# A one-core decoder block on Trainium2: spilled data returned on GpSimd's queue, arithmetic taken off GpSimd, one FFN granule split earlier

## The chip, the cores and the metric

The kernel runs on one core of a Trainium2 chip. The metric is device time in microseconds (us) from the start of the program to its end. Engines are named as in the profile: PE is TensorE (matrix products), PEld its weight loads, DVE is VectorE, ACT is ScalarE, POOL is GpSimd, SP is SyncE, which here only issues transfers. SP, ACT and POOL each have a queue of their own for transfers.

## The reference, cut to what matters

One decoder block in float32 for 512 tokens of width 2048, batch 1: native sparse attention (16 heads of 128, four key/value groups, a compressed, a selected and a sliding-window branch, gated), then a SwiGLU feed-forward net (FFN) of inner width 5632, each behind an RMSNorm, with residual adds and a final RMSNorm.

```python
for i in range(DEPTH):                       # DEPTH = 1
    hn = rmsnorm(h, mix_norm_g[i])
    h = h + nsa_mixer(hn, ...)               # proj = hn @ w_in; ...; o @ w_out
    h = h + swiglu(rmsnorm(h, ffn_norm_g[i]), ffn_w_in[i], ffn_w_out[i])
return rmsnorm(h, final_norm_g)

def swiglu(h, w_in, w_out):
    z = h @ w_in
    a, b = z[..., :D_FF], z[..., D_FF:]
    return (jax.nn.silu(a) * b) @ w_out
```

## The kernel before, in words

**A product.** Every float32 operand is split in two halves: `hi`, its rounded float32r copy, and `lo`, the rest. `three` (L285 to L287) makes one product of three matmuls, hi·hi (L285), one lo with hi (L286), one hi with lo (L287). In a profile row such as `proj<-whi,hn_l` the operands stand behind the arrow.

**Weights** come in granules of 512 KB (128 partitions x 1024 numbers). The class `Weights` keeps three steps apart. `load` (L79) issues the transfer into one of three buffers `raw`, on the queue that `W.queue` names: SP, but POOL while the attention heads run. `split` writes `whi` on ACT (L95) and `wlo`, by a subtraction, on DVE (L99), or on GpSimd when the granule's number is in `on_pool`. The halves go to one of four conversion buffers or, for granules in `W.place`, to a slot of `wr_h`/`wr_l`, which hold them for good. `ahead(n)` splits until n granules stand ready beyond those that PE has taken, and loads up to three more; `take` hands the next one to the matmuls. A raw buffer is filled again only when both parts of its split are done.

**Order.** The order on every engine is the order in which the program calls the instructions; nothing is moved later. Each engine runs its own list in order, and an instruction that waits holds what is behind it on that engine. A transfer's issue counts as such an instruction on the engine whose queue it uses.

**Stages.** (1) First norm and the first projections. (2) The attention heads: `steps(h)` is a list of a head's steps with their places, run between pieces of a second stream, `dense()`, which makes the projections of the coming heads (`qpair`, `kpair`, `vpair`) and then, `N_SPILL` = 6 times, `partial(cb)`: a block of 256 columns of the output projection over heads 0 to 11, added to the input x and stored to DRAM (`d_h`, L722, on POOL). In a head, `turn` transposes the probabilities (L772) into a buffer `turned` and stores it as `d_p` (L773; for the last token tile also `d_pc`, L775); `fetch` reads it back rearranged as `pt` (L779); `part_hi` and `part_lo` split it (L798, `ptl` L808); `values` multiplies it with the value vectors (`o<-ptl,v1h`). The outputs of heads 0 to 10 are stored in DRAM (`d_o`); `reload_o(i)` (L701) brings back four heads (three for i = 2) into `hn_h` and `hn_l`, once the last `qpair`, that of heads 14 and 15, is through with granule i and the place is free.

(3) When the heads are done, `acc`, the residual of 4 token tiles x 2048 columns, is filled: the last 512 columns from x (L890), the first 1536 from `d_h` (L891, 3 MB). `gb2`, the second norm's weights on all partitions (1 MB), is loaded on ACT's queue (L912). The last 512 columns of the output projection over heads 0 to 11 are then made in one block, with `w_out` granules of 2 heads x 512 columns. (4) Token tiles t = 0 to 3: heads 12 to 15 for the four column blocks `cb`, with eight granules split once at t = 0 and held (`w8`; the first six in `wr_h`/`wr_l`). Each block is added to `acc` on DVE (`add`, L895), which frees PE's bank; ACT squares it (L942) into a throw-away bank of PSUM; `rstd` (L230 to L241) makes the norm's factor from the sums; `scaled` multiplies `acc` by factor and `gb2`, three blocks of 512 columns on DVE (L252), the fourth on ACT (L254) and GpSimd (L255). `turned` transposes the tile before this one on PE (L263) and splits the result (`hn_h` on ACT L269, `hn_l` on DVE L274). At a tile's end `W.ahead(min(t, 2))` splits coming granules.

(5) The FFN: three column blocks of 256 plainly (`pp` banks; granules of its first block are numbers #8 to #11 counted from the first held one), during which sums for the rest are prepared; the others as seven products on half-sized blocks (`products`, banks `f0` to `f3`, L1083 on); and the FFN's output projection (L1372 on).

## Time and profile before

| | us |
|---|---|
| median of 3 runs | 2139.99 (2139.48 to 2142.34) |
| the profiled execution | 2138.04 |
| its span, first to last instruction | 2136.2 |
| PE busy in it | 2103.8 (98 %) |
| DVE busy | 1578.0 (74 %) |
| ACT busy | 1001.6 (47 %) |
| POOL busy | 159.8 (7 %) |
| mean granted PE clock | 0.995 |

How to read the views: the page gives busy time per engine over the whole span. A row of the waits is "engine, line, tile <- releaser: us in total, times, longest". A row of the timeline is "start, duration, engine, line, operation, out<-in, shape", and in brackets the engine's idle time before it and what ended that. A row of the chain of waits is "start, duration, what". Matmul rows overlap, since they are pipelined; the spacing of their starts is what one costs. A row such as `raw<-in_nsa_w_out SPq` is a transfer on SP's queue; its last number is the time from issue to landing.

### The profile page before, as it was taken

To read this page: it belongs to the slowest core of one execution; us is meant where nothing else is said; L and a number is where in the kernel's file an instruction comes from. 1 tells how busy PE (TensorE), PEld (TensorE's weight loads), DVE (VectorE), ACT (ScalarE), POOL (GpSimd) and SP (SyncE) were. 2 spreads that over 40 slices of the span, in tenths; PEclk is the share of its full clock that TensorE was granted. 3 is DMA by queue.
4 is the path that set the end of the run, shared out by engine and by line. 5 is a ranking of instruction groups with operands and counts; after the bars stand their busy time and mean duration, and the time that the engine had idled before them with its cause. 6 is when DMAs were issued, how large, how long until landed. Compare 5 with 4: busy or idle time off the path is not lost.

```text
span 2136.2 us, 37530 instructions
## 1 busy us (share of the span) xinstructions
PE 2103.8 (98%) x14821; PEld 1955.8 (92%) x14821; DVE 1578.0 (74%) x2560; ACT 1001.6 (47%) x1629; POOL 159.8 (7%) x233
## 2 busy tenths in 40 slices
PE   8999999999999999999999999999999999999997
PEld 6888898888989978899999999999999888999996
DVE  5565667666656356898888888888888787877776
ACT  5344666666746244444344343443434444444344
POOL 1000111111111121000000000000000000000000
PEclk9999999999999999999999999999999999999999
DMA  6555577766886742343343343443433876878784
GB/s 209 177 159 164 157 201 195 200 187 183 244 259 191 244 161 105 122 139 122 126 130 127 121 126 122 129 129 119 127 121 119 282 277 220 310 262 315 288 312 149
DMA packets 258732, 391.38 MB, mean 183 GB/s; under 512 B 27467, under 2 KB 183163, under 8 KB 257916
## 3 DMA queue, kind: packets, MB, share of 16 engines
q1 hardware_dynamic: 230912, 272.55, 40.6%
q0 software_dynamic: 25648, 112.01, 15.6%
q10 hardware_dynamic: 1996, 4.42, 0.6%
q8 instruction: 116, 1.90, 0.4%
q14 instruction: 60, 0.49, 0.1%
HBM read 323.28 MB, written 70.88 MB: 185 GB/s over the span
## 4 chain that ended last, share of the span: by engine, by line
PE 92%; DVE 3%; DMA 2%; ACT 1%; issue 1%; POOL 0%; ACTq 0%; DVEq 0%; SPq 0%; POOLq 0%
PE f L287 19%; PE f L286 19%; PE f L285 19%; PE proj L285 9%; PE proj L286 8%; PE proj L287 8%; PE o L286 1%; PE o L287 1%; PE s L285 1%; PE o L285 1%; PE s L287 1%; PE s L286 1%; DVE wlo L99 1%; DMA raw<-in_nsa_w_out 1%; DMA d_pc<-turned 1%
## 5 line engine op out<-in xcount | busy, mean ns | idle before, releaser
L99 DVE TENSOR_TENSOR wlo<-raw,whi 128x1024 fp32r<-128x1024 f32 (+1 forms) x223 | 270.3, 1215 | 83.9 <-ACT whi L95 83.8
L95 ACT ACTIVATE whi<-raw 128x1024 fp32r<-128x1024 f32 (+1 forms) x226 | 233.9, 1039 | 200.9 <-DVE raw L968 124.2
L968 DVE TENSOR_TENSOR tlo<-tt,thi 128x1536 fp32r<-128x1536 f32 (+2 forms) x134 | 195.9, 1462 | 110.8 <-ACT thi L1070 88.7
L285 PE MATMUL f<-hn_h,whi 128*128 128x256 f32 x984 | 271.7, 276 | 0.8 <-ACT E L1028 0.8
L287 PE MATMUL f<-hn_h,wlo 128*128 128x256 f32 x984 | 271.6, 276 | 0.0
L286 PE MATMUL f<-hn_l,whi 128*128 128x256 f32 x984 | 271.6, 276 | 0.0
L1065 ACT ACTIVATE whi<-raw 128x1024 fp32r<-128x1024 f32 x123 | 126.1, 1057 | 292.3 <-DVE raw L968 282.1
L285 PE MATMUL proj<-hn_h,whi 128*128 128x512 f32 x512 | 202.8, 396 | 0.3 <-ACT hn_h L419 0.3
L286 PE MATMUL proj<-hn_l,whi 128*128 128x512 f32 x512 | 199.9, 390 | 0.3 <-DVE hn_l L420 0.3
L287 PE MATMUL proj<-hn_h,wlo 128*128 128x512 f32 x512 | 199.9, 390 | 0.0
L285 PEld LDWEIGHTS f<-hn_h,whi 128*128 128x128 f32 x984 | 184.7, 188 | 1.3 <-ACT E L1028 1.3
L287 PEld LDWEIGHTS f<-hn_h,wlo 128*128 128x128 f32 x984 | 184.7, 188 | 0.0
L286 PEld LDWEIGHTS f<-hn_l,whi 128*128 128x128 f32 x984 | 184.7, 188 | 0.0
L285 PE MATMUL proj<-whi,hn_h 128*128 128x256 f32 (+2 forms) x568 | 163.5, 288 | 0.0
L287 PE MATMUL proj<-whi,hn_l 128*128 128x256 f32 (+2 forms) x568 | 162.9, 287 | 0.0
L286 PE MATMUL proj<-wlo,hn_h 128*128 128x256 f32 (+2 forms) x568 | 162.8, 287 | 0.0
L1070 ACT ACTIVATE thi<-tt 128x1536 fp32r<-128x1536 f32 x82 | 121.9, 1487 | 84.0 <-PE f L286 84.0
L968 DVE TENSOR_TENSOR wlo<-raw,whi 128x1024 fp32r<-128x1024 f32 x123 | 147.0, 1223 | 0.0
L287 PE MATMUL f<-whi,tlo 128*128 128x512 f32 x320 | 124.9, 390 | 0.6 <-DVE tlo L968 0.6
L286 PE MATMUL f<-wlo,thi 128*128 128x512 f32 x320 | 125.0, 391 | 0.0
L285 PE MATMUL f<-whi,thi 128*128 128x512 f32 x320 | 124.7, 390 | 0.0
L287 PEld LDWEIGHTS proj<-hn_h,wlo 128*128 128x128 f32 x512 | 96.1, 188 | 21.4 <-DVE wlo L99 0.2
(323 smaller groups left out, 6157.6 us busy)
## 6 DMA issues: line engine op xcount, KB each, us to landing
raw<-in_ffn_w_in SPq DMA_DIRECT2D x135, 512.0 KB, 3.6
raw<-in_ffn_w_out SPq DMA_DIRECT2D x88, 512.0 KB, 5.6
rawx<-in_ffn_w_in SPq DMA_DIRECT2D x41, 512.0 KB, 4.9
rawx<-d_a SPq DMA_DIRECT2D x34, 512.0 KB, 4.9
ah<-d_s POOLq DMA_DIRECT2D x16, 896.0 KB, 7.0
al<-d_s POOLq DMA_DIRECT2D x16, 896.0 KB, 9.1
raw<-in_nsa_w_in SPq DMA_DIRECT2D x24, 512.0 KB, 4.4
raw<-in_nsa_w_in POOLq DMA_DIRECT2D x24, 512.0 KB, 6.1
```

The source lines that it names most:

```text
L95: self.nc.scalar.activation(hi[:, :n], src, AF.Copy)
L99: eng.tensor_tensor(lo[:, :n], src, hi[:, :n].bitcast(F32), op=OP.subtract)
L285: mm(o, ah, bh, start=start, stop=False, skip_group_check=True)
L286: mm(o, ah, bl, start=False, stop=False, skip_group_check=True)
L287: mm(o, al, bh, start=False, stop=stop, skip_group_check=True)
L968: dve.tensor_tensor(o, a, b, op=OP.subtract)
L1065: act(h, r, AF.Copy)
L1070: act(h, ttf, AF.Copy)
```

## The change

1. `reload_o` issues its six transfers on POOL's queue, not SP's, and each pair is called inside the next granule of the last `qpair`, behind its second step.
2. `acc<-d_h` (3 MB) and `gb2` (1 MB) are loaded on POOL's queue, behind the last store of `d_h`; before, on SP's and ACT's.
3. GpSimd does no arithmetic: `on_pool` is gone (all low halves are made on DVE), and `scaled` does all four blocks on DVE.
4. `wr_h`/`wr_l` have seven slots, so that one granule fewer takes a conversion buffer. `W.ahead` at the end of tile t gets (0, 1, 3, 3)[t] instead of (0, 1, 2, 2)[t]: the third FFN granule (#10) is split after t = 2.
5. PSUM: the pool `psx` stays to the end; products and output projection take their first bank from it and f1 to f3 from `pf` (`ffn_banks`).

PE's instructions are the same in number and order; only names of banks and buffers differ. The lines of the changed file are up to 8 lower.

SP's transfers at the end of the last `qpair` before. `d_p_93<-turned_1828` is the store of transposed probabilities of one token tile, `pt` the read back:

```order
L701 DMA hn_h<-d_o 128x4x512
L701 DMA hn_l<-d_o 128x4x512
L773 DMA d_p_93<-turned_1828 128x512
L779 DMA pt_1833<-d_p_94 32x4x64 x4
L773 DMA d_p_92<-turned_1827 128x768
L779 DMA pt_1832<-d_p_93 32x4x128 x4
L701 DMA hn_h<-d_o 128x3x512
L701 DMA hn_l<-d_o 128x3x512
L773 DMA d_p_91<-turned_1826 128x1024
```

and POOL's queue there now (`stage` and `tb` are loads for the first spilled block and for a head's bias):

```order
L694 DMA hn_h<-d_o 128x4x512
L694 DMA hn_l<-d_o 128x4x512
L79 DMA raw<-in_nsa_w_out 128x4x256
L694 DMA hn_h<-d_o 128x4x512
L694 DMA hn_l<-d_o 128x4x512
L79 DMA raw<-in_nsa_w_out 128x4x256
L694 DMA hn_h<-d_o 128x3x512
L694 DMA hn_l<-d_o 128x3x512
L79 DMA raw<-in_nsa_w_out 128x4x256
L700 DMA stage<-in_x 128x4x256
L636 DMA tb<-d_u 128x512
```

The third pair stood on SP directly ahead of a tile's `d_p` (and `d_pc` behind it); now each pair stands on POOL between two raw loads.

DVE from the last spilled block to the first two adds of tile t = 0, before:

```order
L720 TENSOR_TENSOR stage<-stage,proj 128x512
L99 TENSOR_TENSOR wlo<-raw,whi 128x1024 x4
L99 TENSOR_TENSOR wr_l<-raw,wr_h 128x1024 x3
L895 TENSOR_TENSOR acc<-acc,proj 128x512 x2
L895 TENSOR_TENSOR acc<-acc,po 128x512 x2
L99 TENSOR_TENSOR wlo<-raw,whi 128x1024
L895 TENSOR_TENSOR acc<-acc,proj 128x512 x2
```

and now:

```order
L713 TENSOR_TENSOR stage<-stage,proj 128x512
L98 TENSOR_TENSOR wlo<-raw,whi 128x1024 x4
L98 TENSOR_TENSOR wr_l<-raw,wr_h 128x1024 x6
L888 TENSOR_TENSOR acc<-acc,proj 128x512 x2
L888 TENSOR_TENSOR acc<-acc,po 128x512 x2
L98 TENSOR_TENSOR wr_l<-raw,wr_h 128x1024
L98 TENSOR_TENSOR wlo<-raw,whi 128x1024
L888 TENSOR_TENSOR acc<-acc,proj 128x512 x2
```

Six splits of held granules stand ahead of the adds of the column block, where three stood; the other three were on POOL.

DVE from the multiplies of tile t = 2 into t = 3, before:

```order
L252 SCALAR_TENSOR_TENSOR xn<-acc,rs,gb_7617 128x512 x3
L895 TENSOR_TENSOR acc<-acc,proj 128x512 x2
L274 TENSOR_TENSOR hn_l<-pp,hn_h 128x4x128 x2
L895 TENSOR_TENSOR acc<-acc,po 128x512
L274 TENSOR_TENSOR hn_l<-pp,hn_h 128x4x128 x2
```

and now:

```order
L247 SCALAR_TENSOR_TENSOR xn<-acc,rs,gb_7617 128x512 x4
L98 TENSOR_TENSOR wlo<-raw,whi 128x1024 x2
L888 TENSOR_TENSOR acc<-acc,proj 128x512 x2
L266 TENSOR_TENSOR hn_l<-pp,hn_h 128x4x128 x2
L888 TENSOR_TENSOR acc<-acc,po 128x512
```

A fourth multiply and two splits (granules #9 and #10) now stand ahead of the adds of tile t = 3.

The diff:

```diff
--- before.py
+++ after.py
@@ -65,7 +65,7 @@
     def __init__(self, nc, raw, conv, specs):
         self.nc, self.raw, self.conv, self.specs = nc, raw, conv, specs
         self.nd = self.ncv = self.nt = 0
-        self.r, self.c, self.place, self.on_pool, self.sums = {}, {}, {}, set(), {}
+        self.r, self.c, self.place, self.sums = {}, {}, {}, {}
         self.at, self.off = 0, {}
         self.queue, self.late = nc.sync, None
 
@@ -93,10 +93,9 @@
         src = self.r.pop(i).rearrange("p k c -> p (k c)")
         rest = self.sums[i](src) if i in self.sums else None
         self.nc.scalar.activation(hi[:, :n], src, AF.Copy)
-        eng = self.nc.gpsimd if i in self.on_pool else self.nc.vector
 
         def low():
-            eng.tensor_tensor(lo[:, :n], src, hi[:, :n].bitcast(F32), op=OP.subtract)
+            self.nc.vector.tensor_tensor(lo[:, :n], src, hi[:, :n].bitcast(F32), op=OP.subtract)
 
         if self.late is None:
             low()
@@ -193,13 +192,10 @@
     dram = ctx.enter_context(tc.tile_pool(name="dram", bufs=1, space=DRAM))
     front, early = ctx.enter_context(ExitStack()), ctx.enter_context(ExitStack())
     hnp = front.enter_context(tc.tile_pool(name="hnp", bufs=1))
-    psx = early.enter_context(tc.tile_pool(name="psx", bufs=2, space=PSUM))
+    psx = ctx.enter_context(tc.tile_pool(name="psx", bufs=2, space=PSUM))
     specs, specs2, marks, off = granules(w_in, w1k, w1v, w_out, f_in, f_out)
     W = Weights(nc, rawp, convp, specs)
     W.at, W.off = 48, off
-    for m in marks:
-        W.on_pool.update((m + 1, m + 3, m + 5, m + 7))
-    W.on_pool.update((marks[0] + 9, marks[0] + 11))
 
     ident = const.tile([128, 128], F32, name="ident")
     make_identity(nc, ident)
@@ -245,14 +241,10 @@
         run(rstd_steps(ss, y))
         return y
 
-    def scaled(src, y, gb, dst, n_pool):
+    def scaled(src, y, gb, dst):
         for j in range(4):
             c = slice(512 * j, 512 * (j + 1))
-            if j < 4 - n_pool:
-                dve.scalar_tensor_tensor(dst[:, c], src[:, c], y, gb[:, c], op0=OP.mult, op1=OP.mult)
-            else:
-                act(dst[:, c], src[:, c], AF.Copy, scale=y)
-                pool.tensor_tensor(dst[:, c], dst[:, c], gb[:, c], op=OP.mult)
+            dve.scalar_tensor_tensor(dst[:, c], src[:, c], y, gb[:, c], op0=OP.mult, op1=OP.mult)
 
     def transposed(xn, js, tiles):
         ps = []
@@ -664,9 +656,10 @@
             ps = proj2()
             end = q_out(ps, h0)
             for i in range(4):
-                yield from ws(ps, i, W.take(), end=end)
-                if h0 == H - 2 and i < 3:
-                    reload_o(i)
+                for k, _ in enumerate(ws(ps, i, W.take(), end=end)):
+                    if h0 == H - 2 and i and k == 1:
+                        reload_o(i - 1)
+                    yield
 
         def kpair(g):
             ps = proj2()
@@ -698,8 +691,8 @@
         def reload_o(i):
             n = min(4, N_BACK - 4 * i)
             for part, t in enumerate((hn_h, hn_l)):
-                nc.sync.dma_start(t[:, 4 * i:4 * i + n].bitcast(F32),
-                                  d_o[4 * i:4 * i + n, part].rearrange("h p s -> p h s"))
+                pool.dma_start(t[:, 4 * i:4 * i + n].bitcast(F32),
+                               d_o[4 * i:4 * i + n, part].rearrange("h p s -> p h s"))
 
         def partial(cb):
             st = ap_.tile([128, 1024], F32, name="stage").rearrange("p (t c) -> p t c", t=NT)
@@ -888,7 +881,7 @@
     acc = accp.tile([128, NT, D], F32, name="acc")
     spill = 256 * N_SPILL
     nc.sync.dma_start(acc[:, :, spill:], x[:, spill:].rearrange("(t p) c -> p t c", p=128))
-    nc.sync.dma_start(acc[:, :, :spill], d_h.rearrange("(t p) c -> p t c", p=128))
+    pool.dma_start(acc[:, :, :spill], d_h.rearrange("(t p) c -> p t c", p=128))
 
     def add(t, cb, p):
         a = acc[:, t, 512 * cb:512 * (cb + 1)]
@@ -909,11 +902,11 @@
     with tc.tile_pool(name="n2", bufs=1) as n2:
         act(warm, epsc, AF.Sqrt)
         gb2 = n2.tile([128, D], F32, name="gb2")
-        nc.scalar.dma_start(gb2, ffn_g[0:1, :].to_broadcast([128, D]))
+        pool.dma_start(gb2, ffn_g[0:1, :].to_broadcast([128, D]))
         xn = n2.tile([128, D + 64], F32, name="xn")
-        wr_h = n2.tile([128, 6, 1024], F32R, name="wr_h")
-        wr_l = n2.tile([128, 6, 1024], F32R, name="wr_l")
-        for i in range(6):
+        wr_h = n2.tile([128, 7, 1024], F32R, name="wr_h")
+        wr_l = n2.tile([128, 7, 1024], F32R, name="wr_l")
+        for i in range(7):
             W.place[marks[0] + i] = wr_h[:, i], wr_l[:, i]
         for cb in range(N_SPILL // 2, 4):
             po = out_tiles()
@@ -940,8 +933,8 @@
                     turned(xn, (2 * cb - 2, 2 * cb - 1), t - 1)
                 junk = ps3.tile([128, 512], F32, name="pp")
                 act(junk, acc[:, t, 512 * cb:512 * (cb + 1)], AF.Square, accum_out=ss[:, cb:cb + 1])
-            scaled(acc[:, t], rstd(ss), gb2, xn, 1)
-            W.ahead(min(t, 2))
+            scaled(acc[:, t], rstd(ss), gb2, xn)
+            W.ahead((0, 1, 3, 3)[t])
         pa = [ps3.tile([128, 512], F32, name="pp") for _ in range(2)]
         gs = []
         for i in range(4):
@@ -1083,8 +1076,7 @@
     def products(q):
         p, u = q // 2, q % 2
         if not u:
-            banks[p] = [pf.tile([128, 512], F32, name=f"f{i}").rearrange("p (a c) -> p a c", a=2)
-                        for i in range(4)]
+            banks[p] = [x.rearrange("p (a c) -> p a c", a=2) for x in ffn_banks()]
         order = ("p1", "p5", "p2", "p3", "p7", "p6", "p4") if p else ("p1", "p5", "p2", "p7", "p6", "p4", "p3")
         for n in order:
             bh, bl = prod[q][n]
@@ -1157,6 +1149,10 @@
             sub(hn_l[:, k, T2], S4[u], f32(hn_h[:, k, T2]))
     early.close()
     pf = ctx.enter_context(tc.tile_pool(name="pf", bufs=2, space=PSUM))
+
+    def ffn_banks():
+        return [psx.tile([128, 512], F32, name="proj")] + [pf.tile([128, 512], F32, name=f"f{i}")
+                                                           for i in range(1, 4)]
 
     W2 = Weights(nc, rawp, convp, specs2)
     pool.memset(tp.tile([128, TP_GAP], F32, name="gap", bufs=1), 0.0)
@@ -1372,8 +1368,8 @@
     n, na, pending = 0, 1, None
     for b in range(4):
         units = ORDER[b][:-N_TAIL] if b == 3 else ORDER[b]
-        po = [pf.tile([128, 512], F32, name=f"f{i}") for i in range(4)]
-        qs = {x: pf.tile([128, 512], F32, name=f"f{i}") for i, x in enumerate(("p1", "p5", "p6", "p7"))}
+        po = ffn_banks()
+        qs = dict(zip(("p1", "p5", "p6", "p7"), ffn_banks()))
         first7 = next(j for j in units if j in SEVEN[b])
         last7 = [j for j in units if j in SEVEN[b]][-1]
         started = False
```

## The prediction

> **What bounds the kernel now.** First the page's busy shares, then TensorE's list of waits: if TensorE (PE) is nearly full, only its waits can be won.
>
> ```profile
> PE 2103.8 (98%) x14821; PEld 1955.8 (92%) x14821; DVE 1578.0 (74%) x2560; ACT 1001.6 (47%) x1629; POOL 159.8 (7%) x233
> ```
> ```profile
> PE o L286 <- DVE ptl L808: 4.8, 1, 4.8
> PE proj L285 <- issue: 3.2, 1, 3.2
> ...
> PE pp L287 <- DVE wlo L99: 2.7, 1, 2.7
> PE f L285 <- ACT E L1028: 0.8, 1, 0.8
> ...
> PE pp L263 <- DVE hn_l L274: 0.4, 1, 0.4
> ```
> PE is 98 % busy and the change removes no matmul. Four single waits, here called A (4.8), B (3.2), C (2.7) and D (0.8), stand where the diff works. A wait costs more than its idle time: in the windows view (us, then busy time of PE, PEld, DVE, ACT, POOL, then PE's granted clock) the next stretch runs at half clock after A, B and C:
>
> ```profile
> 605.60:609.06 3.46, 1.21 (x11) 1.00 (x9) 0.00 (x0) 0.00 (x0) 0.00 (x0) 1.00 1.03 337
> 609.06:615.88 6.82, 4.32 (x20) 4.32 (x21) 3.58 (x13) 3.38 (x8) 0.76 (x1) 0.50 0.64 171
> 762.66:766.07 3.41, 3.41 (x9) 2.65 (x9) 1.69 (x4) 1.20 (x2) 2.41 (x1) 0.50 0.62 202
> 820.68:824.10 3.42, 0.84 (x7) 0.85 (x8) 3.42 (x3) 0.36 (x1) 1.44 (x1) 1.00 0.00 0
> 824.10:827.51 3.41, 3.41 (x19) 3.41 (x18) 0.30 (x1) 0.00 (x0) 0.00 (x0) 0.50 0.92 303
> ```
> PE's timeline around A, and the chain of waits in the half-clock stretch, give the spacing of like matmuls:
>
> ```profile
> 605.73 0.28 PE L287 MATMUL proj<-whi,hn_l 128*128 128x256 f32 x1
> ...
> 606.53 0.28 PE L285 MATMUL o<-pth,v1h 128*128 128x256 f32 x1
> 611.56 0.58 PE L286 MATMUL o<-ptl,v1h 128*128 128x256 f32 x1 [4.75 <-DVE ptl L808]
> ```
> ```profile
> 615.21 0.21 PE proj L286
> 615.42 0.21 PE proj L287
> ```
> Full clock: seven steps in 0.80, 0.114 each. Half clock: 0.21, so 1−0.114/0.21 = 46 % of busy half-clock time is lost. A: 611.56−606.53−0.114 = 4.92 late, which is 0.17 over its idle time; I add 0.17 to the other waits too. Half clock after A: 4.32×0.46 = 1.99; after B and C 3.41×0.46 = 1.57 each. So **A = 6.91, B = 3.37+1.57 = 4.94, C = 2.87+1.57 = 4.44, D = 0.97**, together 17.26.
>
> **Part by part.** *Reload of hn (A).* SP's timeline, the chain, the DMA table (last column: median us to landing) and DVE's timeline:
>
> ```profile
> 596.03 0.38 SPq L701 DMA_DIRECT2D hn_h<-d_o  x1
> ```
> ```profile
> 597.52 13.11 DMA d_pc<-turned
> ```
> ```profile
> d_pc<-turned SPq DMA_DIRECT2D x16, 64.0 KB, 2.8
> ```
> ```profile
> 610.72 0.48 DVE L772 STREAM_TRANSPOSE turned<-p 128x288 f32<-128x288 f32 x1 [7.05 <-DMA d_pc<-turned]
> ```
> The third reload pair (3 heads, 1.5 MB) goes out directly ahead of the 512 KB d_p and the 64 KB d_pc on SP. d_pc lands after 13.11 instead of 2.8; the transpose that reuses its buffer waits, then ptl, then PE. The transpose sat idle 7.05 and PE lost 4.92, so A is gone if d_pc lands 4.92 earlier, by 605.7, in 8.2. On POOL the pair follows this raw load:
>
> ```profile
> 593.01 0.75 POOL L79 DMA_DIRECT2D raw<-in_nsa_w_out  x1 [9.04 <-DVE turned L772]
> ```
> so it goes out at about 593.8, three us before d_p. From 593 POOL's queue then has two raw blocks (1 MB), the pair (1.5), a stage (0.5) and a tb (0.25): 3.25 MB. At the 337 GB/s of the first window that ends at 602.7; if all of it went ahead of SP, d_p and d_pc (0.58 MB, 1.7 us) would land at 604.4 (6.9 us); if SP gets half, at 601 (3.4). Both are under 8.2. I take A as gone. The three pairs are six more issues on POOL, of 0.75 or less by the row above, on a queue that sat idle 9 us there. Each pair waits until PE has finished a granule of qpair, and stands behind a raw load that comes after that, so it holds nothing up: the raw loads queued behind it are for granules well ahead of PE. The first partial block needs the third pair's heads only in its last granule, some 12 us after 593.8. If this cover fails, PE waits for the pair itself, at most as long as for d_pc now.
>
> The Trainium skill speaks against this edit: DMA: Bandwidth & Descriptors ("Issuing engines are not separate DMA queues") says that DMAs started from any engine share the same 16 engines, so that another issuer saves only issue time. By it the bytes still collide and A stays (a rival below); the trace's stall, though, is order within one queue, which the move does change.
>
> *acc<-d_h and gb2 (B).* From the chain of waits and DVE's timeline:
>
> ```profile
> 736.47 0.35 ACTq L912
> ...
> 740.41 11.64 DMA raw<-in_nsa_w_out
> ```
> ```profile
> 760.37 1.23 DVE L99 TENSOR_TENSOR wr_l<-raw,wr_h 128x1024 fp32r<-128x1024 f32 x1 [3.60 <-ACT wr_h L95]
> 761.52 1.28 DVE L895 TENSOR_TENSOR acc<-acc,proj 128x512 f32<-128x512 f32 x2
> ```
> ACT stands on gb2's issue and SP on acc<-d_h's until the last spilled block has landed at 736.4; then 4 MB run ahead of the raw loads. The sixth place granule (raw #5) ends at 761.6, and the adds that free PE's banks stand behind its split.
>
> With both loads on POOL, nothing on ACT or SP waits for d_h. The splits then go as PE frees conversion buffers, one granule (48 matmuls×0.114 = 5.5 us) after the other: I place them at 727, 732 and 737.5, and the raw loads #0 to #4 that take the emptied raw buffers between 730 and 742. What is new is that these share the engines with POOL's 4.2 MB (3 MB of acc, 1 MB of gb2) from 737:
>
> ```profile
> DMA packets 421, 2.53 MB, mean 422 GB/s; under 512 B 9, under 2 KB 9, under 8 KB 420
> ```
> ```profile
> q0 software_dynamic: 291, 1.19, 97.5%
> q1 hardware_dynamic: 17, 0.03, 3.0%
> ```
> ```profile
> q0 software_dynamic: 134, 0.55, 67.6%
> q1 hardware_dynamic: 133, 0.27, 35.0%
> ```
> The first is 741.5 to 747.5, the others 1678 to 1681 and 1681 to 1683, where POOL (q0) loads beside SP (q1). If the queues alternate packets as in the last pair, SP has 0.27 MB in 2 us, 135 GB/s: raws #2 to #4, from 740, take 3.9 us each until 751.5, and #5, with the engines to itself from 752.3 (POOL's 4.2 MB at 275), lands at about 753.5. If POOL's bytes all go first (737 to 747 at 422), four raws of 0.52 MB follow in 5.0, with about 2 us to landing: 754. My estimate is between. It must land by 755.9: ACT 1.06, DVE 1.23 and an add of 0.68 later (1.28 for two) is 758.9, when PE wants the bank. B is gone at both ends, with about 2 us to spare; against it, six splits now precede the adds on DVE, three before, and a wait there holds every later split, add and multiply.
>
> *No arithmetic on GpSimd, third granule early (C, t=2).*
>
> ```profile
> 819.83 3.38 DVE L99 TENSOR_TENSOR wlo<-raw,whi 128x1024 fp32r<-128x1024 f32 x1
> ```
> ```profile
> 819.60 2.52 POOL L99 TENSOR_TENSOR wlo<-raw,whi 128x1024 fp32r<-128x1024 f32 x1 [0.24 <-POOL xn L255]
> ```
> C is the third granule's split on DVE, which took 3.38 instead of the 1.23 of the row at 760.37, while GpSimd split another granule. The third granule is now split a tile earlier, and the fourth, behind t=3's multiplies, finds GpSimd idle and ends on DVE 2.1 earlier than 823.2, ahead of PE: C is gone. The moved multiply is free for the same reason:
>
> ```profile
> L252 DVE SCALAR_TENSOR_TENSOR xn<-acc,rs,gb x12: 744/750/1784, 778.1 to 818.1; 128x512 f32<-128x512 f32 x12
> ```
> ```profile
> 804.12 3.11 DVE L252 SCALAR_TENSOR_TENSOR xn<-acc,rs,gb 128x512 f32<-128x512 f32 x3
> ```
> The third multiply takes 1.78 beside GpSimd's; the two before take 3.11−1.78 = 1.33, 0.67 each, so four alone take 2.75 with the pipeline's end, less than 3.11. The 0.4 wait at t=2 should shrink by 0.3.
>
> *What it adds: t=3.* Two splits (1.1 to 1.2 each) now stand on DVE between t=2's multiplies and the adds: xn ends at 806.9, the splits at 809.1, two adds at 810.4, and by my estimate the Square at 810.6 and hn_l's first half at 811.9. PE wants these banks for its second transposes:
>
> ```profile
> 810.05 1.03 PE L263 MATMUL pp<-ident,xn 128*128 128x128 f32 x8
> ```
> The first four need a bank free at 810.6, the next one at 812 against 810.5. Below nothing it cannot go (no wait stands there now); above, 3 us if the delay of the splits (2.4) and of the banks add. I take 1.5, between, since the matmuls behind can start when one bank is free. Half clock would add 1.57: A, B and C had under 1.3 us of work in 3.41, and a 1.5 us wait leaves 1.9; the 0.8 of D was followed by none.
>
> The Trainium skill, TensorE: Matmul & The Clock Gate ("Why this matters for your kernels"), puts the drop at gaps over about 3 us; C's 2.7 tripped it, so the rule is too loose here, and the row decides. By the rule t=3 would stay at 1.5 even at the upper bound.
>
> *PSUM (D).* The first product's bank was the one that ACT's E had still to empty; now it is one free since the token tiles. The third product, 1.4 later, needs ACT's at about the time it is ready: D is gone, between 0 and 0.97; I take 0.97.
>
> **Sum.** −17.26−0.3+1.5 = **−16.1**. Against the profiled execution's own 2138.04 (span 2136.2, 1.84 around it) that is 2121.9; the runs' median, 2139.99, is 1.95 above it, which gives **2124**. Later, PE stays the bound and splits run 1 to 3 us ahead of it, so the gain reaches the end. All small bounds together (t=3 from 0 to 4.6, D from 0.97 to 0): 2122 to 2128, the forecast's own range.
>
> **The rivals.**
> R1, B stays: six splits or POOL's 4 MB make raw #5 late by the spare 2 plus 3.4. For: the 97.5 % row. Against: ACT starts 10 us earlier. 2124+4.9 = 2129.
> R2, A stays: POOL's packets hold d_p and d_pc beyond 8.2. For: 6.9 at the one end leaves 1.3. Against: 3.4 at the other. 2124+6.9 = 2131.
> R3, the waits only move (the change doesn't do what it says): A and B stay and t=3 costs 3: 2124+6.9+4.9+1.5+1.57 = 2139.
> R4, slower: POOL's loads go ahead of SP's and are slow themselves, as
>
> ```profile
> acc<-d_r POOLq DMA_DIRECT2D x1, 2048.0 KB, 13.0
> ```
> has 157 GB/s. Then 4.2 MB end at 763.7, raw #2 lands at 765, is split by 767.3, and raw #5 (0.52 MB, 3.3 us at that rate) takes its buffer and lands at 770.6: 14.7 late, and 1.6 of half clock. At A, 3.25 MB end at 613.7: 8+2. Time 2124+16.3+10 = 2150. With raw #5 after 770.3 the change is, at B alone, no longer faster. Against it: in the 97.5 % row POOL moved 1.19 MB in 3 us, 397 GB/s.
>
> **How the numbers follow.** Forecast 0.60 (2124), R1 0.15 (2129), R2 0.12 (2131), R3 0.08 (2139), R4 0.05 (2150). A measurement tells some 0.2 % (4.3 us) from no change: the first three are faster, 0.87; R3 the same, 0.08; R4 slower, 0.05. The range goes from 2119 (three below the lowest bound, about the runs' spread) to 2134, three above R2, and leaves out R3 and R4.
>
> **What would show it.** Right: no PE wait above 1 us between 606 and 766; d_pc under 8 us; ACT splitting at 727 and raw #5 landed by 755.9; no DVE split above 1.3 near 820; the four xn at 2.75; a wait of 0 to 3 near 810 and full clock there. Wrong: half clock at 609 (A) or 763 (B), SP's packets near 3 % while POOL loads, or a new wait of PE behind DVE's splits.

## The result, and the profile after

The changed kernel takes 2125.27 us, median of six runs (2124.15 to 2133.42), beside 2139.93 before; the ratio is 0.9939 (0.9929 to 0.995). The forecast of 2124 and its range hold. Two later sets of runs of the same kernel, in the experiments, gave 2131.12 (0.9967, 0.9956 to 0.9978) and 2127.39 (0.9943, 0.9931 to 0.9955): all 18 executions lie between 2124.2 and 2137.3 with a median of 2129.3. The gain is 8 to 15 us (14.7, 7.7 and 11.8 in the three sets); the sum of 16.1 was the best case. One execution of one experiment, the run with both edits, took 5028 us, more than twice any other, and is not counted. What takes the difference can be seen, since the profiled execution is the longest of the six: 2133.42, span 2131.3.

PE's waits in it, by line (L277 to L279 are now the three matmuls of `three`):

```profile
PE o L277 <- ACT pth L791: 2.4, 2, 1.9
PE proj L277 <- issue: 2.0, 1, 2.0
```

C (2.7) and D (0.8) are gone from the list; another wait of 2.7 in it stands at the end of the program, where it was 2.8 before. A has turned into two waits of 2.4 together, of another releaser, and B went from 3.2 to 2.0 only. The windows view says the same by the clock (columns as in the prediction):

```profile
614.97:618.38 3.41, 3.29 (x14) 3.10 (x14) 3.22 (x13) 3.41 (x10) 0.00 (x0) 0.50 0.75 201
...
761.74:765.16 3.42, 3.42 (x10) 2.65 (x9) 2.37 (x4) 1.10 (x2) 0.00 (x0) 0.50 0.76 250
817.00:820.40 3.40, 3.40 (x31) 3.40 (x31) 3.40 (x6) 0.71 (x2) 0.00 (x0) 1.00 0.39 161
820.40:823.80 3.40, 3.40 (x32) 3.40 (x31) 1.21 (x3) 0.78 (x2) 0.00 (x0) 1.00 0.49 154
```

Half clock is still paid behind A and B, no more behind C, where PE now has 31 and 32 matmuls in each stretch.

**What is left of A.** SP's and DVE's timelines, the chain of waits there, and the share of the queues from 600 to 606 (q0 is POOL's, q1 SP's; packets, MB, share):

```profile
594.91 0.41 SPq L768 DMA_DIRECT2D d_pc<-turned  x1
```
```profile
608.18 0.48 DVE L765 STREAM_TRANSPOSE turned<-p 128x288 f32<-128x288 f32 x1 [0.92 <-DMA d_pc<-turned]
```
```profile
597.10 12.88 DMA pt<-d_p
...
610.05 4.07 DMA pc<-d_pc
614.12 0.52 ACT pth L791
```
```profile
q0 software_dynamic: 485, 1.82, 86.6%
q1 hardware_dynamic: 406, 0.30, 16.8%
```

d_pc holds DVE for 0.9, not 7.05. It was not faster: it landed at 608.1, 13.2 after its issue, as against 13.1 before. It was issued earlier: 594.91 against 597.52, although PE is 1.8 later at this place than before (the start of the program took longer). And the small reads behind it, pt and pc, run beside POOL's reload, raw, stage and tb. The queues alternate almost packet by packet (485 to 406), but SP's packets there are small: 0.30 MB in 6 us, 50 GB/s. pt takes 12.88, and pc is issued late.

**What is left of B.** The chain, DVE's timeline, and the queues from 740 to 744 (POOL's alone) and from 744 to 750:

```profile
739.87 11.25 DMA raw<-in_nsa_w_out
751.15 1.07 ACT wr_h L95
752.24 1.23 DVE wr_l L98
753.49 4.75 DMA raw<-in_nsa_w_out
758.26 1.07 ACT wr_h L95
```
```profile
756.73 3.86 DVE L98 TENSOR_TENSOR wr_l<-raw,wr_h 128x1024 fp32r<-128x1024 f32 x3 [3.26 <-ACT wr_h L95]
760.50 1.28 DVE L888 TENSOR_TENSOR acc<-acc,proj 128x512 f32<-128x512 f32 x2
```
```profile
q0 software_dynamic: 193, 1.19, 87.9%
```
```profile
q0 software_dynamic: 278, 1.71, 74.4%
q1 hardware_dynamic: 270, 0.53, 25.4%
```

ACT and SP are no longer held: the splits and the first raw loads go out as forecast. But raw #2, issued at 739.87, lands at 751.1 behind POOL's 4 MB, its split frees the buffer for #5 at 753.5, and #5 lands at 758.2, when it was needed by 755.9. From 740 to 744 SP's queue moved nothing; then packets alternate (278 to 270), but POOL's carry 1.71 MB/278 = 6 KB each and SP's 2 KB: 0.53 MB in 6 us, 88 GB/s. The three splits in the row at 756.73 are those of #3, #4 and #5. PE starts when the first add behind them has freed its bank, 0.8 after that add begins (761.28).

**C and the tile stage.** DVE's timeline, and the multiplies (ns, least, median, most):

```profile
805.16 2.35 DVE L98 TENSOR_TENSOR wlo<-raw,whi 128x1024 fp32r<-128x1024 f32 x2
...
819.19 1.22 DVE L98 TENSOR_TENSOR wlo<-raw,whi 128x1024 fp32r<-128x1024 f32 x1
```
```profile
L247 DVE SCALAR_TENSOR_TENSOR xn<-acc,rs,gb x16: 743/744/753, 777.0 to 818.5; 128x512 f32<-128x512 f32 x16
```

No split takes longer than 1.23, and none of the 16 multiplies longer than 0.753; four fit in the 2.74 that was forecast as 2.75. At tile 3 PE's timeline has the new wait:

```profile
808.20 0.39 PE L279 MATMUL po<-wr_h,hn_l 128*128 128x512 f32 x1
808.92 0.66 PE L255 MATMUL pp<-ident,xn 128*128 128x128 f32 x4 [0.34 <-ACT pp L935]
810.13 0.65 PE L255 MATMUL pp<-ident,xn 128*128 128x128 f32 x4 [0.56 <-DVE hn_l L266]
810.54 0.48 PE L277 MATMUL po<-wr_h,hn_h 128*128 128x512 f32 x1
```

From the last product to the first behind the transposes it is 2.34; before it was 810.84−809.82 = 1.02. The price is 1.3, and no half clock follows.

### The profile page after: what moved, and what is told of

The parts are those of the page before. It is cut to its first block, busy times and chain, and to the rows that moved or that the text cites. A ratio compares the mean times of both kernels' runs of the same rounds, so it can differ in the third digit from the quotient of the medians.

```text
span 2131.3 us, 37517 instructions
## 1 busy us (share of the span) xinstructions
PE 2105.6 (99%) x14821; PEld 1955.4 (92%) x14821; DVE 1580.3 (74%) x2570; ACT 998.3 (47%) x1625; POOL 143.5 (7%) x231
## 4 chain that ended last, share of the span: by engine, by line
PE 94%; DMA 3%; DVE 2%; ACT 1%; issue 0%; ACTq 0%; DVEq 0%; SPq 0%
PE f L278 14%; PE f L277 14%; PE proj L277 14%; PE f L279 14%; PE proj L279 14%; PE proj L278 14%; PE pp L279 1%; PE pp L278 1%; PE pp L277 1%; PE o L278 1%; PE s L277 1%; PE o L279 1%; PE s L279 1%; PE s L278 1%; PE o L277 1%; DMA raw<-in_nsa_w_out 1%
## 5 line engine op out<-in xcount | busy, mean ns | idle before, releaser
L277 PE MATMUL proj<-hn_h,whi 128*128 128x512 f32 (+1 forms) x840 | 294.3, 350 | 0.1
L278 PE MATMUL proj<-hn_l,whi 128*128 128x512 f32 (+1 forms) x840 | 291.4, 347 | 0.0
L279 PE MATMUL proj<-hn_h,wlo 128*128 128x512 f32 (+1 forms) x840 | 291.3, 347 | 0.0
L278 PE MATMUL f<-hn_l,whi 128*128 128x256 f32 x656 | 181.2, 276 | 0.0
L279 PE MATMUL f<-hn_h,wlo 128*128 128x256 f32 x656 | 181.2, 276 | 0.0
L277 PE MATMUL f<-hn_h,whi 128*128 128x256 f32 x656 | 181.2, 276 | 0.0
L279 PEld LDWEIGHTS proj<-hn_h,wlo 128*128 128x128 f32 x840 | 158.1, 188 | 21.4 <-DVE wlo L98 0.2
L277 PEld LDWEIGHTS proj<-hn_h,whi 128*128 128x128 f32 x840 | 158.4, 189 | 17.8 <-ACT hn_h L411 0.5
L278 PEld LDWEIGHTS proj<-hn_l,whi 128*128 128x128 f32 x840 | 158.3, 188 | 17.6 <-DVE hn_l L412 0.5
L277 PE MATMUL proj<-whi,hn_h 128*128 128x256 f32 (+2 forms) x568 | 163.5, 288 | 0.0
L279 PE MATMUL proj<-whi,hn_l 128*128 128x256 f32 (+2 forms) x568 | 162.9, 287 | 0.0
L277 PEld LDWEIGHTS f<-hn_h,whi 128*128 128x128 f32 x656 | 123.2, 188 | 0.0
L279 PEld LDWEIGHTS f<-hn_h,wlo 128*128 128x128 f32 x656 | 123.2, 188 | 0.0
L752 ACT ACTIVATE p<-p,ms 128x31 f32<-128x31 f32 (+2 forms) x192 | 90.5, 472 | 43.7 <-DVE ms L750 40.8
```

Source lines behind the costliest of these rows:

```text
L277: mm(o, ah, bh, start=start, stop=False, skip_group_check=True)
L278: mm(o, ah, bl, start=False, stop=False, skip_group_check=True)
L279: mm(o, al, bh, start=False, stop=stop, skip_group_check=True)
L752: act(p, p, AF.Exp, bias=s["mx"][:, t, i:i + 1], scale=-1.0, accum_out=s["sm"][:, t, i:i + 1])
```

## The experiments

Each is an edit of the changed kernel, unless said. A difference in time below about 3 us between two of them is not told by their runs, whose executions spread by 4 to 9 us; then the rows of the waits decide.

### The changed kernel once more, twice

> The changed kernel as it is, once more. Its six executions fell in two groups: 2124.2 to 2125.5 (four) and 2130.5 and 2133.4, and the profiled one is the slowest, with what is left of waits A (0.5 and 2.1 us at 608 and 612, half clock 1.6) and B (2.2 us at 759, half clock 1.6): 7.9 us together. Theory 1 (what is left of A and B is a matter of how the queues of SP and POOL share the DMA engines in that execution): executions near 2125 have no half clock at 615 and 762, slower ones have one or both; if a fast one is profiled, its spans show raw #5 landed before 755.9 and d_p and the loads behind it in well under 10 us. Rival 1 (both waits are in every execution, and the slow group is something else): a profile of an execution near 2125 shows the same 0.5, 2.1 and 2.2 us waits, and the sum of the prediction came out right by chance.

Measured 2131.12 (seven runs, 2128.18 to 2137.31). The profiled execution (2132.72) has no wait of PE at all between 600 and 620, so the wait at A can be wholly gone; but B is larger, 4.1. The wait, ACT's timeline and DVE's:

```profile
PE proj L277 <- ACT wr_h L95: 4.1, 1, 4.1
```
```profile
755.92 1.06 ACT L95 ACTIVATE wr_h<-raw 128x1024 fp32r<-128x1024 f32 x1 [0.26 <-DMA raw<-in_nsa_w_out]
```
```profile
755.69 2.54 DVE L98 TENSOR_TENSOR wr_l<-raw,wr_h 128x1024 fp32r<-128x1024 f32 x2 [3.48 <-ACT wr_h L95]
758.15 1.28 DVE L888 TENSOR_TENSOR acc<-acc,proj 128x512 f32<-128x512 f32 x2
```

The list names ACT as releaser, but PE starts at 758.94, 0.8 after the first of these adds begins, as in the first profile. The two splits ahead of the adds are those of raws #4 and #5. PE comes to the place at 754.4, 4.4 earlier than in the first profile (758.9), since A no longer holds it; raw #5 lands at 755.9, 2.3 earlier only. B's end is set by the transfers, so what A gives is in part paid back at B.

> The changed kernel once more, beside the two that follow. Its profiles so far show wait B at 2.2 and at 4.3 us, with raw #5 issued at 752.2 to 753.5 and landed at 757.2 to 758.2. Theory (the raw loads get too small a share beside POOL's 4 MB: POOL's packets are 6144 bytes and SP's 2048, one to one, about 97 GB/s for SP): B again 2 to 4.5 us and half clock 1.6, time 2128 to 2133. Rival (the first six executions, 2125 in four, are what the kernel does as a rule): B below 0.5 us, 2125.

Measured 2127.39 (2125.28 to 2130.27), just under the 2128 expected, with waits of 1.0 near 610 and 2.2 at B and half clock behind B alone. The issue at 752.2 and the landing at 757.2 that the expectation takes for raw #5 of the second profile are those of raw #6, whose split stands behind the adds. Raw #5 was issued at 741.65 there and landed at 755.9; here it landed at 753.4. The theory of the share holds: from 742 to 748 the queues moved 321 packets and 1.92 MB against 322 and 0.63 (105 GB/s for SP). Rival 1 of the first run falls for A, whose rest was 2.4, 0 and 1.0; B was in all three profiles. No execution near 2125 of this kernel was profiled; what those hold stays open.

### Undoing the reload

```diff
-                pool.dma_start(t[:, 4 * i:4 * i + n].bitcast(F32),
+                nc.sync.dma_start(t[:, 4 * i:4 * i + n].bitcast(F32),
```
and the call behind its granule, as before.

> The changed kernel with the reload pairs back on SP's queue, each behind its granule of the last qpair, as before. Theory (wait A is order within SP's queue): d_pc lands after some 13 us again, PE waits 4.9 us near 606 and runs 4.3 us at half clock: 2125 + 6.9 = 2132. Rival (the move to another queue does nothing, the bytes collide on the same DMA engines anyway): what the changed kernel has left at this place and no more, 2125 to 2129, and the profile shows d_pc no later than in the changed kernel's.

Measured 2134.76 (eleven runs). The median is 3.6 above the changed kernel's 2131.12 on the same chip, but the intervals of the two ratios overlap (0.9966 to 0.9984 and 0.9956 to 0.9978), so the rows decide. PE's wait, SP's waits from 575 to 603, and the chain:

```profile
PE o L278 <- DVE ptl L800: 5.5, 1, 5.5
```
```profile
SPq L771 <- DMA d_p<-turned: 9.9, 2, 5.1
```
```profile
599.47 13.71 DMA d_pc<-turned
```

A is back: ptl waits for d_pc, PE stands 5.5, and the rival, that another queue does nothing, falls. That d_pc takes 13.7 is no sign of it, since it took 13.2 in the changed kernel's first profile too. What tells them apart is the issue: 599.47 here, 594.91 there, with the transpose before it at 594.0 in both. On SP stores d_p stand behind reload pairs, the reads pt wait for these stores (9.9 in two waits), and the next store stands behind the reads. The price on the whole is not 6.9: B was 2.0 in this profile, against 4.1 in the one beside it. The two waits are not independent.

### Undoing the loads of acc and gb2

```diff
-    pool.dma_start(acc[:, :, :spill], d_h.rearrange("(t p) c -> p t c", p=128))
+    nc.sync.dma_start(acc[:, :, :spill], d_h.rearrange("(t p) c -> p t c", p=128))
-        pool.dma_start(gb2, ffn_g[0:1, :].to_broadcast([128, D]))
+        nc.scalar.dma_start(gb2, ffn_g[0:1, :].to_broadcast([128, D]))
```

> The changed kernel with acc<-d_h back on SP's queue and gb2 back on ACT's, as before. Theory (wait B is the raw loads and splits held behind these two): raw #5 lands near 759 again, PE waits 3.2 us at 758.9 and runs 3.4 us at half clock: 2125 + 4.9 = 2130. Rival (six splits ahead of the adds on DVE, three before, cost by themselves): 1.2 us or more on top, PE waits 4.5 us or more, 2131 to 2133. Rival 2 (the queue makes no difference, 4 MB collide either way): 2125, as the changed kernel.

Measured 2134.07 (eleven runs). The median is 3 above the changed kernel's, and again the intervals overlap (0.9968 to 0.9986 here). PE waits 5.4 at B; the wait, ACT's and DVE's timelines, and GpSimd's of before:

```profile
PE proj L277 <- ACT wr_h L95: 5.4, 1, 5.4
```
```profile
756.83 1.06 ACT L95 ACTIVATE wr_h<-raw 128x1024 fp32r<-128x1024 f32 x1 [0.25 <-DMA raw<-in_nsa_w_out]
```
```profile
756.61 2.53 DVE L98 TENSOR_TENSOR wr_l<-raw,wr_h 128x1024 fp32r<-128x1024 f32 x2 [2.15 <-ACT wr_h L95]
759.06 1.28 DVE L888 TENSOR_TENSOR acc<-acc,proj 128x512 f32<-128x512 f32 x2
```
```profile
762.88 2.41 POOL L99 TENSOR_TENSOR wr_l<-raw,wr_h 128x1024 fp32r<-128x1024 f32 x1 [2.71 <-ACT wr_h L95]
```

The wait is in the size that the rival named (4.5 or more), and its reason is right in part. That PE is there at 754.2 instead of 758.8 is not it: the last store of `d_h` landed 4.7 earlier too (731.6 against 736.4), and the loads follow it. But the adds now stand behind the split of raw #5, which landed at 756.8. Before, they stood behind #4's, and #5's was GpSimd's, at 762.88, after the adds. Without #5's split they could have begun at 757.8 (756.61 and one split of 1.23), 1.2 of the 2.2 by which this wait is longer than before's 3.2. It is not the row of six that costs: DVE sat idle 2.15 ahead of the last two. Counted from PE's last matmul ahead of B to one behind the half clock, this kernel loses 3.3 against before, where the changed kernel's three profiles have −1.2, +0.7 and −1.1 (and two experiments below with the same loads, the third granule's old place and the old PSUM banks, −0.1 and −3.2). So the move of the two loads is worth some 2.6 to 6.5 at this place, and rival 2, that the queue makes no difference, falls.

### GpSimd's arithmetic back

```diff
+            (self.nc.gpsimd if i in self.on_pool else self.nc.vector).tensor_tensor(lo[:, :n], src, hi[:, :n].bitcast(F32), op=OP.subtract)
...
+            if j < 3: ...                      # DVE, as now
+            else: act(dst[:, c], src[:, c], AF.Copy, scale=y); pool.tensor_tensor(...)
```

> The changed kernel with GpSimd's arithmetic back: low halves of the granules 1, 3, 5, 7, 9 and 11 of the held and first FFN granules, and the fourth multiply of each tile, on GpSimd; the third FFN granule stays split a tile ahead. Theory (wait C came from the third granule's split on DVE standing beside a GpSimd split; split a tile ahead, it is off the path): C stays gone, only small waits come and go (0.4 at t = 2 back, that at t = 3 smaller since one of the two splits is off DVE): 2125, within 2. Rival (it is GpSimd's arithmetic itself that slows DVE everywhere in the stage): C or its like returns, 2.7 us at the fourth granule and half clock 1.6, 2129.

Measured 2129.68 (four runs, 2126.29 to 2134.36), not told from the changed kernel. The waits, DVE's timeline and the window behind it:

```profile
PE pp L262 <- ACT pp L942: 1.7, 1, 1.7
PE pp L262 <- DVE hn_l L273: 1.1, 2, 0.6
```
```profile
798.99 3.42 DVE L98 TENSOR_TENSOR wlo<-raw,whi 128x1024 fp32r<-128x1024 f32 x1
```
```profile
805.92:809.33 3.41, 3.41 (x10) 2.63 (x9) 1.44 (x3) 1.07 (x3) 0.00 (x0) 0.50 0.09 32
```

C at the fourth granule stays gone, as the theory said. But the wait at tile 3 did not shrink, as it expected: the slow split went along with the third granule, 3.42 on DVE beside a GpSimd split of 2.86. PE waits 1.7 and 0.6 there (0.3 and 0.6 in the changed kernel), a half-clock stretch follows, and tile 3 costs 4.3 and not 1.3. That is the rival's price, at another place than it said. So the cause of C is the pair of splits, and moving one a tile ahead moves the cost.

### The third granule at its old place

```diff
-            W.ahead((0, 1, 3, 3)[t])
+            W.ahead((0, 1, 2, 2)[t])
```

> The changed kernel with the third FFN granule split where it was, after tile 3's multiplies, with no arithmetic on GpSimd. Two splits (the third and the fourth granule) then stand one behind the other on DVE, from 819.5 on a clock of before, done at about 820.8 and 822. Theory (C came from the split that took 3.38 beside a GpSimd split): the third granule's low half is ready at 820.8, some 0.5 us after PE wants it at 820.4: PE waits 0.5 us, no half clock; the waits at t = 3 (0.2 and 0.7 us in the changed kernel) go: the changed kernel's time within 1. Rival (C is the place of the split, and the early split is what mends it): PE waits 2 us or more at the third granule and half clock follows, 3 to 4.4 us slower than the changed kernel.

Measured 2129.95 (2124.93 to 2130.27), 2.6 above the changed kernel's 2127.39 beside it where within 1 was expected; the intervals overlap (0.9936 to 0.996 and 0.9931 to 0.9955), and B is 3.1 in its profile. DVE's timeline at the end of tile 3, and PE's at the third granule:

```profile
813.02 2.35 DVE L98 TENSOR_TENSOR wlo<-raw,whi 128x1024 fp32r<-128x1024 f32 x2
```
```profile
813.89 0.28 PE L278 MATMUL pp<-hn_l,whi 128*128 128x256 f32 x1
814.30 0.39 PE L279 MATMUL pp<-hn_h,wlo 128*128 128x256 f32 x1
```

Both splits together take 2.35, less than one of them did beside GpSimd. PE is 814.30−813.89−0.12 = 0.3 late, without half clock, and tile 3 costs 0.2 and not 1.3. The rival falls: with GpSimd quiet, the early split saves 0.4 at C and costs 1.1 at tile 3.

### The old PSUM banks

```diff
-    psx = ctx.enter_context(tc.tile_pool(name="psx", bufs=2, space=PSUM))
+    psx = early.enter_context(tc.tile_pool(name="psx", bufs=2, space=PSUM))
...
-        return [psx.tile([128, 512], F32, name="proj")] + [pf.tile([128, 512], F32, name=f"f{i}")
-                                                           for i in range(1, 4)]
+        return [pf.tile([128, 512], F32, name=f"f{i}") for i in range(4)]
```

> The changed kernel with its PSUM banks as before: psx closed after the token stage, f0 to f3 of products and output projection from one pool. Theory (D was the first product's bank, which ACT's E had still to empty): PE waits 0.8 us at the first product again and nothing else changes, 1.0 us slower than the changed kernel; against the changed kernel's runs (2127.4 and 2131.1 here) it cannot be told by the times, so the row of the wait decides: 0.8 us for PE on ACT's E. Rival (the wait went for another reason, the splits that no longer stand on GpSimd): no such wait.

```profile
PE f L277 <- ACT E L1021: 0.7, 1, 0.7
```

The wait D is back at 0.7; the time (2129.34, 2128.53 to 2132.67) cannot show it. The theory holds. The profiled execution took 2129.38 although it has no wait near 610 and no half clock there or at B. So theory 1 of the first run, that slower executions have one or both, is not the whole: here the start and the end of the program cost 4 more than in before's profile.

### acc and gb2 in pieces behind the raw loads

The 4 MB go on SP's queue, cut by token tile: tile 0 behind raw #4, gb2 behind #5, tiles 1 to 3 behind #6 to #8.

```diff
+    def back(t):
+        nc.sync.dma_start(acc[:, t, :spill], d_h[128 * t:128 * (t + 1)])
+    for n in range(NT):
+        W.then[marks[0] + (4, 6, 7, 8)[n]] = lambda n=n: back(n)      # called behind that load
...
+        W.then[marks[0] + 5] = lambda: nc.sync.dma_start(gb2, ffn_g[0:1, :].to_broadcast([128, D]))
```

> The changed kernel with acc<-d_h cut into its four token tiles and, with gb2, put on SP's queue behind the raw loads #4, #5, #6, #7 and #8 (tile 0 behind #4, gb2 behind #5, tiles 1 to 3 behind #6 to #8), so that nothing runs beside raws #2 to #4 and at most 0.75 MB stands ahead of #5. Theory (B is the share of the DMA engines that 4 MB of POOL take from the raw loads): raws #2 to #4 land by 747, #5 by 752, PE waits less than 0.5 us near 755 and stays at full clock: 4 to 6 us less than the changed kernel beside it, 2124 to 2127. Rival (the bytes of this stretch are the bound, in whatever order): the wait moves to the adds of tile 0 or to raw #6, PE stands 2 us or more somewhere between 755 and 790 and the time is that of the changed kernel within 2.

Measured 2125.96 (2121.96 to 2128.83), ratio 0.9933 (0.9921 to 0.9945). The profiled execution has no wait of PE at all between 740 and 800, and between 600 and 2000 half clock from 612.2 to 615.6 alone. DVE's timeline shows raw #5's split done at 751.7 and the adds, one by one, waiting for PE and not PE for them:

```profile
750.52 1.23 DVE L101 TENSOR_TENSOR wr_l<-raw,wr_h 128x1024 fp32r<-128x1024 f32 x1 [1.95 <-ACT wr_h L98]
751.66 0.68 DVE L895 TENSOR_TENSOR acc<-acc,proj 128x512 f32<-128x512 f32 x1
752.93 0.69 DVE L895 TENSOR_TENSOR acc<-acc,proj 128x512 f32<-128x512 f32 x1 [0.59 <-PE proj L282]
```

B is gone with the same bytes through the same DMA engines: it was what ran beside raws #2 to #5 and when. The rival falls. Two things changed at once, the place of the 4 MB behind the urgent loads and their queue; late pieces on POOL's queue were not tried. The median is 1.4 below the changed kernel's beside it, less than the 4 to 6 expected; the intervals overlap, and A's rest (1.5 and half clock in this profile) is in it.

> As the run with pieces, and acc<-in_x (1 MB) also moved, from ahead of raw #0 to behind raw #1. Theory: raw #0 and the last store of d_h land 2 us earlier, but raw #5 is not early because of them (it waits for a buffer), so the same time as with pieces, within 1. Rival (the stretch from 725 to 757 is bound by bytes): 1 to 2.5 us less than with pieces, if B is not gone there.

Measured 2124.87 (2124.12 to 2132.86), 0.9936 (0.9923 to 0.9949): the same, as the theory had it.

> The run with pieces, and the third FFN granule split where it was before the change (after tile 3's multiplies). Theory: the two are at different places and add: no wait near 755, none of the 0.2 and 0.7 us at tile 3 that the changed kernel shows, none at the third granule; what is left is wait A (0 to 3.7 us with half clock, from one execution to the next): 0.8 us less than pieces, 2124 to 2126. Rival (with B gone DVE comes under pressure at the third granule): PE waits there over 1 us, 2127 or more.

Measured 2125.5 (median of the four executions counted, 2123.86 to 2129.93), ratio 0.9935 (0.9922 to 0.9949). In its profile (2127.05) A is 1.3 without half clock, B and the waits at tile 3 are gone. By the rows the two edits add; by the times they are not told from pieces.

### The load of x later

```diff
-            pool.dma_start(st, x[:, c].rearrange("(t p) c -> p t c", p=128))
             for i in range(3):
                 w = W.take()
+                if i == 1:
+                    pool.dma_start(st, x[:, c].rearrange("(t p) c -> p t c", p=128))
```

> The run with both, and each spilled block's load of x (stage, 512 KB) issued before its second granule and not before its first. In the changed kernel the first such load stands on POOL directly behind the third reload pair, at 598 to 600, and SP's small transfers (pt, pc) beside POOL's loads get some 50 GB/s. Theory (what is left of A is the share that POOL's bytes leave to these): with 0.5 of 2.25 MB less on POOL between 594 and 609, pc<-d_pc lands some 1 to 2 us earlier: the wait near 610 falls to 0 to 1.5 us, mostly without half clock, 1 to 3 us less than both, 2121 to 2124. Rival (A is set by the third pair alone, or the load of x is now late for its add): as both, or slower by what the add waits.

Measured 2134.4 (eight runs), 9 above the run with both: a miss on the other side, and the rival's second half. Near 610 the wait is still 1.1, and a new one stands at a later head. PE's wait and DVE's timeline there:

```profile
PE o L281 <- DVE ptl L805: 5.5, 3, 5.0
```
```profile
705.42 0.69 DVE L717 TENSOR_TENSOR stage<-stage,proj 128x512 f32<-128x512 f32 x1 [10.82 <-DMA stage<-in_x]
```

The load of x is now late for its add. It goes out behind a raw load and lands after 9.8, at 705.3; DVE stands 10.8 at the add, ptl stands behind the add on DVE, and PE waits 5.0 and loses two half-clock stretches. In the run with both the same load lands after 5.7, and that add waits for PE. The reads pt and pc land late there too (pc at 705.9); how much of the 5.0 is theirs was not separated.

### Without the third reload pair

> The run with both, without the third reload pair: heads 8 to 10 are not brought back, so the spilled blocks and the last column block multiply what the places of these heads held before; all matmuls stay. Theory (what is left of A is POOL's reload beside SP's small transfers): 1.5 MB less on POOL between 594 and 609, no wait over 0.3 us and no half clock between 600 and 620, and 2121 to 2122.5. Rival (the delay comes from the first two pairs, at 577 to 600, or from the chain of transfers itself): waits of 1 us or more stay near 610.

Measured 2125.23 (2122.39 to 2125.99, four runs). PE has no wait above 0.3 between 600 and 760 and no half clock there. That fits the theory but doesn't show it: four profiles that keep all three pairs (the changed kernel's second, and those with the loads undone, with GpSimd's arithmetic and with the old PSUM banks) have no wait near 610 either. What the row of queues does show is that SP's small transfers got more, 0.47 MB from 600 to 606 instead of 0.30. The time came out above the 2121 to 2122.5 expected; half clock near the end of the program was twice as long as in the first profile (below).

## Why the prediction was right, and where not

The time was inside the range, but by less gain than the sum. That the first median lies 1.3 from the forecast is luck in part: the next two sets gave 2131 and 2127, and the median of all 18 executions lies 5 above it. For each step the start of the same matmul was compared in two timelines, the profiled kernel's and before's; a step is the change of that difference across it.

| step | forecast | first profile | second | third | with pieces and the old split place (both) |
|---|---|---|---|---|---|
| A | −6.9 | −1.7 | −6.3 | −5.4 | −5.2 |
| B and tile 2 | −5.2 | −1.7 | +0.3 | −1.5 | −5.5 |
| tile 3 | +1.5 | +1.3 | +1.3 | +1.3 | +0.2 |
| C | −4.4 | −4.0 | −4.0 | −4.0 | −3.7 |
| D | −1.0 | −0.9 | −0.9 | −0.9 | −0.9 |
| sum | −16.0 | −7.0 | −9.6 | −10.4 | −15.1 |

(Each entry is rounded by itself. The last column has, in C, what the splits cost at their old place.) Beside these the start of the program cost 0.4 to 2.3 more and the end 0.3 to 2.1 more than in the execution profiled before, in parts that the change does not touch (last section).

**A was right that the order in SP's queue was the cause, and wrong in what the move does to the store.** Undone, the step across A is +0.8; with the move it is −1.7, −6.3 and −5.4. The sum took d_pc's issue as it was and its flight as shorter: 3.4 to 6.9, with 8.2 allowed. The flight was 13.2 in the first profile, 8.2 and 7.7 in the other two, against 13.1 before. What came in all three is an earlier issue, 4.6 by the undone run, which the sum left out: issued at 597.5 as before, a flight of 13.2 would have landed d_pc at 610.7, where it landed before (610.6). The reads behind d_pc, pt and pc, were not costed either: at 50 GB/s beside POOL they end the wait in the first profile. Rival R2 is what this profile shows in part; in the second profile it is not there. Over the ten profiles that keep the three pairs on POOL and the load of x in its place, the step across A runs from −0.5 to −7.0; what decides between them stays open. The Trainium skill's rule that another issuer saves only the time of issuing (DMA: Bandwidth & Descriptors, "Issuing engines are not separate DMA queues") is too strong by the undone reload, 5.5 against 0 to 2.4, since an issue can be held back by what stands ahead of it; but the bytes did collide, as it says.

**B failed**: the term of −4.9 came out at −1.2, +0.7 and −1.1 in the three profiles (B alone, without tile 2). The step at fault is "SP has 0.27 MB in 2 us, 135 GB/s". It was taken from a row in which POOL's packets carried 4 KB (0.55 MB in 134); acc<-d_h has rows of 6 KB, and the share was 88 GB/s. Raw #2 then lands at 751 and not 744, and #5, which needs its buffer, at 758.2 and not 753.5; the 2 us to spare were not there. (At 88 GB/s alone raw #2 would take 6 us of the 11.3; 4 more are the stretch from 740 to 744 in which SP's queue moved nothing, and why it did not is open.) The Trainium skill says that each DMA engine goes round robin between its queues, a packet at a time (DMA: Bandwidth & Descriptors, "Queues, rings and completion order"); the 278 to 270 of this trace agree, and what follows, that the larger packets take the larger share of the bytes, is the 1.71 to 0.53 MB.

A row was misread as well: the split that ends at 761.6 is raw #4's and not #5's, which stood on GpSimd at 762.88, behind the adds. So the change makes the adds wait for one granule more; in the first profile #5 landed 1.3 after #4, and a split takes 1.2. R1, given 0.15, is near what happened: its 2129 is the median of all 18 executions, and both reasons that it names, POOL's 4 MB and the six splits, have a part. With acc and gb2 behind the raw loads the same six splits cost PE nothing, and the step across B is −5.1 in all three profiles, near the −4.9 of the forecast.

**A and B were added as if independent.** In the second profile A is gone and PE comes to B 4.4 earlier than in the first, raw #5 only 2.3; 2.1 of A's gain were paid back there.

**C, D, tile 3 and the fourth multiply were right**, each within 0.5 of its term. C's reason was right too, its remedy half: quieting GpSimd alone mends it (the third granule at its old place), the early split alone moves it (GpSimd's arithmetic back), and both together pay 1.1 at tile 3 for 0.4 at C.

R3 and R4 did not come: POOL's 3 MB took 13.1 us, but its share was 74 %, not all.

**A version without B**: pieces, or pieces with the split at its old place, 0.9933 and 0.9935 of before. Against the changed kernel the times (medians of 2125 to 2126 beside 2127) do not settle that it is faster; the missing wait speaks for it.

## What to carry to other kernels

When a load is moved to another queue to get it out of a FIFO, work out the share of bytes, not of packets, that each queue will have, with the packet sizes of the tensors at hand; a deadline two microseconds off is no margin for that estimate. Ask of a transfer in a FIFO both when it is issued and how long it flies: moving its neighbour away changed the first here in every profile, the second not in every one. Put bulk that is needed late behind the urgent loads in the same queue, in pieces, rather than beside them in another. And do not add the gains of two waits on one path before asking whether the second's end is set by something that the first doesn't hold.

## What the runs showed of the hardware that was not expected

The same code at the start of the program ran at two speeds. The windows from 16 to 20 us, before and of the changed kernel's first profile, where nothing is changed:

```profile
16.00:20.00 4.00, 3.72 (x16) 2.55 (x17) 3.85 (x6) 3.97 (x7) 2.16 (x4) 1.00 1.03 375
```
```profile
16.00:20.00 4.00, 4.00 (x9) 2.48 (x10) 3.94 (x6) 3.97 (x7) 2.14 (x4) 1.00 1.04 380
```

PE makes 16 matmuls in the one and 9 in the other. The column says 1.00 in both, but like matmuls start 0.23 us apart in the first and 0.43 in the second, as at half clock; by 20.5 us it has cost 1.9. At the end of the program the wait of 2.7 to 3.2 on the last split (not touched) is followed by one half-clock stretch in the first profile and by two in that of pieces:

```profile
2093.60:2097.00 3.40, 1.97 (x4) 1.27 (x5) 2.17 (x2) 0.00 (x0) 0.00 (x0) 0.50 0.00 0
2097.00:2100.40 3.40, 3.40 (x10) 2.62 (x9) 1.60 (x4) 0.73 (x3) 0.00 (x0) 0.50 0.00 0
```

Such differences come and go between the three profiles of the changed kernel itself: the start was slow in two, and the end had two half-clock stretches in one. That they hang on where a fixed 3.4 us stretch falls against the work was only argued from the lengths (3.41 and 6.82), not shown. The length of a wait alone does not decide: 1.5 near 610 in the run with pieces was followed by half clock, 1.9 at B in the run with GpSimd's arithmetic was not.

A low-half split on DVE takes 1.22 alone and 3.38 to 3.42 beside a GpSimd split of the same size, which itself takes 2.5 to 2.9 there and 2.4 otherwise: two splits side by side took nearly as long as three in a row on DVE.
